# The second group's first tile picks its experts in three steps between its lists

## The chip, the cores and the metric

The kernel runs on one core of one Trainium2 chip. Its metric is the device time of one execution in microseconds (us); less is better. A core has engines with instruction streams of their own: TensorE (PE) for matrix products, VectorE (DVE), ScalarE (ACT), GpSimd (POOL), and SyncE (SP), which here only starts transfers. Sixteen DMA engines move data between the chip's main memory (HBM) and the core's own memory. Here POOL does nothing but start gathered transfers, in which each of 128 partitions fetches a row of its own; SP and ACT start the plain ones.

## The reference, cut to what matters

The reference is one decoder block for 1024 tokens of width 1024. Three token mixers run side by side on a normalised input, are gated and summed, and go through an output projection. A channel mixer follows, in which each token picks 128 experts out of 16384; each expert is one row of `u` and one of `v`:

```python
q = (hf @ w_q).reshape(T, 8, 2, 128)
sc = einsum('thpd,hpkd->thpk', q, subkeys)       # 8 heads x 2 halves x 128 keys
s1, i1 = top_k(sc[:, :, 0], 16)
s2, i2 = top_k(sc[:, :, 1], 16)
cand = (s1[..., :, None] + s2[..., None, :]).reshape(T, 8, 256)
cand_idx = (i1[..., :, None] * 128 + i2[..., None, :]).reshape(T, 8, 256)
top_s, pos = top_k(cand, 16)
idx = take_along_axis(cand_idx, pos, axis=-1)    # 8 x 16 = 128 experts of a token
gate = softmax(top_s)
...
act = gelu(einsum('chkd,cd->chk', u[ic], hc))
out = einsum('chk,chkd->cd', gc * act, v[ic])
```

All of it is float32, and every expert row has 1024 numbers (4096 bytes).

## The kernel before

**Tiles and groups.** The 1024 tokens are eight tiles of 128 (one token per partition), numbered 0 to 7. The dense front (projections, the three mixers, gating, output projection, and the scores of the experts' keys) runs in three groups of 2, 3 and 3 tiles: 0-1, 2-4 and 5-7 (`GROUPS`, line 30; `phase1`, line 1077). "Group 0, 1, 2" below are these. In the code a group is known by its first tile: n0 = 0, 2 or 5.

**Two ways through the experts.** Tiles 4 and 6 (`DENSE`, line 31) take all 16384 experts as a dense product with a matrix of gates; that stage (`dense`, line 1297) comes after the three groups. The other six tiles gather. For each of the 128 chosen experts of a tile, POOL fetches one row of `u` per token (128 rows of 4096 bytes in one instruction, line 1135, called "a row" in the prediction), DVE multiplies it by the token's vector `h` and sums (line 1186), and 34 steps later (`VLAG`) POOL fetches the row of `v`, which PE sums, four at a time, into `poa` and `pob` with weights `wz` (line 1220). `u` has five buffers (`UP`), `v` eight (`VP`), and `h` one (line 1148): the next tile's `h` is loaded over SP when its first row is asked for, once the tile before has no product left.

**The choice.** `select` (line 884) runs at the end of each group. For each of 16 half heads (`hp`) it projects with `w_pq`, forms the scores with the subkeys, copies them to the tile `sc` (or to a `wide` buffer for the second tile of three), and for the group's first tile (for two tiles in the last group) makes the list of the 16 best (`half_list`, `top16`, lines 950 and 875); after every second half head the 112 candidate sums of that head are formed and their 16 best found, with their positions in `pos`. The steps are queued in a small pipe (`Pipe`, line 59), so that the list of `hp` is written two projection steps after its projection. `pick` (line 976) then turns positions into expert numbers: a copy of the indices to float (`f16`), some fifteen small integer and float operations, and one-hot compare, multiply and reduce over eight and over sixteen columns, for each half. `pick` works on a range of heads h0 to h1.

**Stages.** `STAGES` (line 973) cuts the eight heads into three ranges: 0-4, 4-6 and 6-8. In groups 0 and 2 the first tile's ranges are picked inside `select`, as soon as the lists of those heads stand (after hp = 7 and 11); after the first range `begin` (line 906) makes the expert numbers of the first 64 rows and enters the tile in the list `ready` with a limit of 31 rows (`FIRST`, line 47). The last range is picked in `topk` (line 1010), which also makes the gates, turns the indices for the `v` rows and lifts the limit to 128. In group 1 (n0 = 2) `select` only makes the lists of its first tile, tile 2; `topk` picks all eight heads at once, and only at its end tile 2 enters `ready`. The lists of a group's further tiles are made in `topk` as well. `topk` runs as side work, a step now and then, while the next group's front goes on.

**What sets the order.** The loop at lines 1507-1527 weaves three things into one program: steps of the gathered experts (`Experts.step`: a product, a fetch of `v`, sums), steps of the dense front (`fill`), and side work. It keeps two clocks of estimated time, one for PE and one for DMA, and a due time that grows with each expert step, and adds front steps until PE's clock has passed the others. When no expert step is possible it runs a front step, and side work until the next tile is ready. ACT and POOL run in the order in which the program was written; for PE, DVE and SP a scheduler of the framework arranges the instructions by when their inputs are expected.

Of the kernel before, what the change touches and what calls it, by code (L numbers as in the profile page):

```python
# [7 lines left out]
F32 = mybir.dt.float32  # L8
# [11 lines left out]
NT = T // 128  # L20
# [61 lines left out]
def block_kernel(ctx: ExitStack, tc: tile.TileContext, io):  # L82
# [6 lines left out]
    tk = pool("tk", 1)  # L89
# [22 lines left out]
    def bank():  # L112
        return ps.tile([128, 512], F32, name="bank")
# [124 lines left out]
    def load(out, src):  # L238
        count(out)
        nc.sync.dma_start(out, src)  # L240
# [99 lines left out]
    def proj_T(w, h, n):  # L340

        p = bank()
        if type(w) is tuple:
            wh, wl = w
            for k in range(KD):
                hh, hl = (x[:, k % 4, :n] for x in h[1][k // 4])
                mmr(p[:, :n], wh[:, k, :], hh, start=k == 0, stop=False)
                mmr(p[:, :n], wl[:, k, :], hh, start=False, stop=False)
                mmr(p[:, :n], wh[:, k, :], hl, start=False, stop=k == KD - 1)
            return p  # L350
        for piece, o, m in pieces(h[0], n):
            for k in range(KD):
                mm(p[:, o:o + m], w[:, k, :], piece[:, k], start=k == 0, stop=k == KD - 1)
        return p
# [529 lines left out]
    def select(pipe, weights, h2T, n0, G, out):  # L884
        N = G * 128
        sides(9999)
        subk = big.tile([128, 16, 128], F32, name="big")
        load(subk, io["subk"])
        scs = [wide.tile([128, 8 * NMAX], F32, name="wide")[:, :2048].rearrange("p (a b) -> p a b", a=16)
               if G > SUB and i == 1 else sc.tile([128, 16, 128], F32, name="sc") for i in range(G)]  # L890
        lists = [new_lists()]
        last = n0 + G == NT
        if last or n0 == 0:
            early[:] = [tk.tile([128, 8, 2, 16], F32, name="f16")]
        if last:

            a, b = (gm.tile([128, 2, 2, 128], F32, name="ab") for _ in range(2))
            half = lambda t: t.rearrange("p h (a b) -> p (h a) b", b=16)
            early.append(half(b[:, 1]).rearrange("p (h z) b -> p h z b", z=2))
            a, c, b = a[:, 0], a[:, 1], b[:, 0]  # L900
            lists.append((half(a).rearrange("p (h z) b -> p h z b", z=2),
                          half(b).rearrange("p (h z) b -> p h z b", z=2).bitcast(U32),
                          half(c)[:, 0:8], half(c)[:, 8:16].bitcast(U32)))
        entry = {}

        def begin(room, sel, m):
            idx = room[:, 896:896 + m]
            nc.vector.scalar_tensor_tensor(idx, sel[:, 0, :m], 128.0, sel[:, 1, :m], op0=OP.mult, op1=OP.add)
            iI = keep.tile([128, 128], I32, name="iI", bufs=3)
            nc.vector.tensor_copy(iI[:, :m], idx)  # L910
            entry.update(n=n0, iI=iI, have=m, limit=FIRST)
            out.append(entry)

        for hp in range(16):
            p = proj_T(weights("w_pq", hp), h2T, N)
            q = tmp.tile([128, EW], F32, name="e")
            actf(q[:, :N], p[:, :N], AF.Copy)

            def part(hp=hp, q=q):
                z = bank()  # L920
                for i in range(G):
                    mm(z[:, i * 128:(i + 1) * 128], q[:, i * 128:(i + 1) * 128], subk[:, hp, :],
                       start=True, stop=True)
                for i in range(G):
                    actf(scs[i][:, hp, :], z[:, i * 128:(i + 1) * 128], AF.Copy)

            def first(hp=hp):
                for l, x in zip(lists, scs):
                    half_list(hp, x, *l)
                for f, l, x in zip(early, lists, scs):  # L930
                    for h0, h1, at in STAGES[:-1]:
                        if (last or n0 == 0) and hp == 2 * h1 - 1:
                            room = x.rearrange("p a b -> p (a b)")
                            sel = None
                            for sel in pick(room, l, f, h0, h1, at):
                                pass
                            if h0 == 0 and l is lists[0]:
                                begin(room, sel, 16 * h1)
            pipe.tick()
            pipe.push(part, first)  # L940
            next(stores[n0], None)
            yield
        pipe.flush()
        side.append(topk(n0, G, scs, out, lists, entry))

    def new_lists():
        return (tk.tile([128, 8, 2, 16], F32, name="s16", bufs=2), tk.tile([128, 8, 2, 16], U32, name="i16"),
                tk.tile([128, 8, 16], F32, name="ts"), tk.tile([128, 8, 16], U32, name="pos"))
# [23 lines left out]
    early = []  # L972
# [37 lines left out]
    def topk(n0, G, scs, out, lists, entry):  # L1010
        for i in range(G):
            if i >= len(lists):
                l = new_lists()
                for hp in range(16):
                    half_list(hp, scs[i], *l, tied=n0 + G == NT)
                    yield
                    if hp % 2:
                        yield
            else:
                l = lists[i]  # L1020
            s16, i16, ts, pos = l
            room = scs[i].rearrange("p a b -> p (a b)")
            flat = lambda t: t.rearrange("p h a -> p (h a)")
            if i >= len(lists) or 0 < n0 < NT - G:
                f16 = tk.tile([128, 8, 2, 16], F32, name="f16")
                sel = yield from pick(room, l, f16, 0, 8, (1792, 1664, 0, 0, 512, 1536))
            else:
                sel = yield from pick(room, l, early[i], *STAGES[-1])
            idx = room[:, 1024:1152]
            nc.vector.scalar_tensor_tensor(idx, sel[:, 0, :], 128.0, sel[:, 1, :], op0=OP.mult, op1=OP.add)  # L1030
            ge = s16.rearrange("p h a b -> p (h a b)")[:, 0:128].rearrange("p (a b) -> p a b", a=8)
            nc.vector.tensor_sub(ge, ts, ts[:, :, 0:1].to_broadcast([128, 8, 16]))
            actf(ge, ge, AF.Exp)
            sm = room[:, 1152:1160]
            nc.vector.tensor_reduce(sm, ge, AX, OP.add)
            nc.vector.reciprocal(sm, sm)
            shared = sm[:, :, None].to_broadcast([128, 8, 16])
            if n0 + i in DENSE:
                nc.vector.tensor_mul(ge, ge, shared)
            else:  # L1040
                begun = i == 0 and bool(entry)
                t = entry if begun else dict(n=n0 + i, iI=keep.tile([128, 128], I32, name="iI", bufs=3), have=0)
                nc.vector.tensor_copy(t["iI"][:, t["have"]:], idx[:, t["have"]:])
                gk = keep.tile([128, 128], F32, name="gk", bufs=3)
                nc.vector.tensor_mul(gk.rearrange("p (a b) -> p a b", a=8), ge, shared)
            for _ in range(LAG):
                yield
            pt = pg.tile([128, 512], F32, name="pt") if behind[0] else bank()
            if n0 + i in DENSE:
                flip(pt[:, 0:128], sel[:, 0, :])  # L1050
                flip(pt[:, 128:256], sel[:, 1, :])
                flip(pt[:, 256:384], flat(ge))
                sl = gm.tile([128, 3, 128], F32, name="sl", bufs=1)
                actf(sl, pt[:, :384].rearrange("p (a b) -> p a b", a=3), AF.Copy)
                chosen.append(sl)
                stored.append(n0 + i)
                yield
                continue

            for i4 in range(4):  # L1060
                turn(pt[:, i4 * 32:i4 * 32 + 32], idx[:, 32 * i4:32 * i4 + 32])
            iT = keep.tile([128, 4, QB, 4], I32, name="iT", bufs=3)
            nc.vector.tensor_copy(iT.rearrange("p c j i -> p i c j"),
                                  pt[:, :128].rearrange("p (i c j) -> p i c j", i=4, c=4))
            t.update(gk=gk, iT=iT, limit=128)
            if not begun:
                out.append(t)
            yield
# [388 lines left out]
    def sides(n):  # L1457
        while n and side and not wait[0]:
            if next(side[0], 0) == 0:
                side.pop(0)  # L1460
            n -= 1
# [122 lines left out]
```

## Time and profile before

| what | value |
|---|---|
| median of 3 runs | 3554.88 us (3551.26 to 3556.88) |
| the profiled execution | 3549.93 us |
| its span | 3548.2 us |
| instructions in the span | 56579 |
| mean granted clock of TensorE | 0.942 |
| read from HBM / written | 1140.61 MB / 37.75 MB |
| mean DMA rate over the span | 332 GB/s |

The profile is of one execution. Its page gives the busy time of each engine (PE for matrix products, PEld for their weight loads), the DMA queues, and the chain of work that ended last, followed back from the end. Finer views are used beside it: a timeline of one engine's instructions (start, duration, engine, line, operation, output and inputs, and in brackets the idle time before it and what ended that), groups of equal instructions (count, busy time, mean duration in ns), and stretches of the span with each engine's busy time. Names of tiles lose their numbers there: `i` is `i16`, `s` is `s16`, `f` is `f16`. Each matrix product of float32 appears as more than one record.

### The profile page before, as it was taken

What the parts mean: (1) busy time and instruction counts of PE and PEld (TensorE: products, weight loads), DVE (VectorE), ACT (ScalarE), POOL (GpSimd) and SP (SyncE); (2) the same over time, 40 slices, a digit from 0 to 9 for tenths busy, and PEclk for the clock granted to TensorE, in tenths of its full rate; (3) what the DMA queues carried; (4) which work ended last, traced back from release to release, by engine and by line L of the source; (5) the groups of instructions that cost most, each with busy time, mean ns of one, the idle gap of its engine ahead of it and who ended that gap; (6) DMA issues with size and microseconds to landing.
All of it is one profiled execution on the core that took longest, in us unless ns stands there. A gap on an engine that the chain in (4) does not pass through costs nothing.

```text
span 3548.2 us, 56579 instructions
## 1 busy us (share of the span) xinstructions
PE 3134.6 (88%) x21218; PEld 2270.9 (64%) x21218; DVE 2304.0 (65%) x5883; ACT 1015.4 (29%) x2075; POOL 1745.9 (49%) x1543
## 2 busy tenths in 40 slices
PE   7999968899899899899998999886768888898998
PEld 5889835566455476566664555565547777787876
DVE  6544587565544457888666665578759766667673
ACT  4543213332200111344222111112223333333332
POOL 0000045564567654667665665444754645354653
PEclk9999989999999999999999999988989999999999
DMA  4435677898899998899998999988998999999997
GB/s 169 122 104 178 220 280 279 308 401 319 298 372 400 409 392 320 308 330 344 400 334 309 376 397 385 403 299 311 400 382 334 372 407 388 377 386 409 406 404 293
DMA packets 344611, 1182.13 MB, mean 333 GB/s; under 512 B 38481, under 2 KB 81489, under 8 KB 324881
## 3 DMA queue, kind: packets, MB, share of 16 engines
q0 software_dynamic: 221184, 805.40, 59.9%
q1 hardware_dynamic: 100848, 336.37, 25.5%
q10 hardware_dynamic: 22304, 36.74, 2.8%
q8 instruction: 167, 2.74, 0.3%
q14 instruction: 108, 0.88, 0.1%
HBM read 1140.61 MB, written 37.75 MB: 332 GB/s over the span
## 4 chain that ended last, share of the span: by engine, by line
PE 51%; DMA 15%; DVE 12%; issue 12%; POOL 6%; ACT 2%; another core or an unknown queue 1%; ACTq 0%; SPq 0%; POOLq 0%; DVEq 0%
PE bank L120 33%; PE bank L1241 10%; DMA u<-in_u,iI 8%; DMA v<-in_v,iT 4%; PE poa L1220 4%; DVE u L1186 4%; POOL v L1135 3%; PE pob L1220 3%; POOL u L1135 3%; PE bank L124 1%; DMA ur<-in_uT 1%; ACT e L131 1%; DVE sc L880 0%; DVE ab L1271 0%
## 5 line engine op out<-in xcount | busy, mean ns | idle before, releaser
L1135 POOL DMA_INDIRECT u<-in_u,iI x768 | 876.8, 1142 | 961.3 <-DVE pos L879 437.6
L1186 DVE SCALAR_TENSOR_TENSOR u<-u,h 128x1024 f32<-128x1024 f32 x768 | 932.5, 1220 | 514.2 <-DMA u<-in_u,iI 428.9
L1135 POOL DMA_INDIRECT v<-in_v,iT x768 | 868.3, 1131 | 805.7 <-PE pob L1220 319.1
L120 PE MATMUL bank<-wide,w 128*128 128x384 f32 x1536 | 520.9, 492 | 3.1 <-DVE wide L816 3.0
L120 PEld LDWEIGHTS bank<-wide,w 128*128 128x128 f32 x1536 | 290.5, 192 | 208.8 <-issue 21.0
L1241 PE MATMUL bank<-hh,pu 128*128 128x256 f32 x1200 | 234.6, 295 | 37.6 <-ACT w L131 28.5
L1220 PE MATMUL poa<-v,wz 128*32 128x256 f32 x3072 | 220.0, 410 | 45.2 <-DMA v<-in_v,iT 24.9
L1241 PE MATMUL bank<-pv,wh 128*128 128x512 f32 x712 | 232.4, 407 | 23.0 <-DVE pv L1336 12.0
L131 ACT ACTIVATE e<-bank 128x512 f32<-128x512 f32 (+2 forms) x208 | 110.1, 529 | 486.0 <-PE bank L120 345.8
L120 PE MATMUL bank<-w,wide 128*128 128x128 f32 (+1 forms) x1056 | 221.6, 367 | 25.6 <-DVE wide L336 23.4
L120 PE MATMUL bank<-big,w 128*128 128x256 f32 (+1 forms) x1280 | 237.7, 343 | 2.5 <-issue 2.5
L1220 PE MATMUL pob<-v,wz 128*32 128x256 f32 x3072 | 205.7, 399 | 36.8 <-DVE u L1186 17.1
L1241 PEld LDWEIGHTS bank<-hh,pu 128*128 128x128 f32 x1200 | 201.6, 202 | 52.2 <-ACT w L131 31.1
L120 PEld LDWEIGHTS bank<-big,w 128*128 128x128 f32 x1280 | 207.9, 194 | 30.7 <-issue 9.8
L120 PEld LDWEIGHTS bank<-w,wide 128*128 128x128 f32 x1056 | 143.7, 193 | 99.9 <-issue 66.7
L1220 PEld LDWEIGHTS poa<-v,wz 128*32 128x32 f32 x3072 | 97.3, 116 | 140.2 <-issue 47.0
L1220 PEld LDWEIGHTS pob<-v,wz 128*32 128x32 f32 x3072 | 96.4, 113 | 125.8 <-issue 47.3
L1241 PE MATMUL bank<-hl,pu 128*128 128x256 f32 x600 | 175.7, 293 | 0.0
L1241 PEld LDWEIGHTS bank<-pv,wh 128*128 128x128 f32 x712 | 131.5, 193 | 59.9 <-DVE pv L1336 14.3
L131 ACT ACTIVATE w<-bank 128x256 f32<-128x256 f32 x128 | 48.7, 381 | 385.1 <-PE bank L1241 244.1
L120 PE MATMUL bank<-oT,w 128*128 128x384 f32 (+1 forms) x480 | 153.6, 459 | 2.5 <-DMA w<-in_w_o 2.5
L1241 PE MATMUL bank<-u 128*128 128x256 f32 (+1 forms) x464 | 146.6, 316 | 9.6 <-ACT u L131 9.6
(306 smaller groups left out, 5565.3 us busy)
## 6 DMA issues: line engine op xcount, KB each, us to landing
ur<-in_uT SPq DMA_DIRECT2D x64, 1024.0 KB
vr<-in_vd SPq DMA_DIRECT2D x64, 1024.0 KB
w<-in_w_in SPq DMA_DIRECT2D x90, 512.0 KB
w<-in_w_gate SPq DMA_DIRECT2D x72, 512.0 KB
w<-in_w_pq SPq DMA_DIRECT2D x48, 512.0 KB
g<-gd SPq DMA_DIRECT2D x16, 1024.0 KB
w<-in_w_o SPq DMA_DIRECT2D x48, 256.0 KB
w<-in_w_out SPq DMA_DIRECT2D x24, 512.0 KB
```

The costliest lines, as they stand in the source:

```text
L120: nc.tensor.matmul(out, lhsT, rhs, **kw)
L124: nc.tensor.transpose(out, in_, ident)
L131: nc.scalar.activation(out, in_, f, **kw)
L1135: nc.gpsimd.indirect_dma_start(out=t, out_offset=None, in_=io[kind], in_offset=bass.IndirectOffsetOnAxis(ap=ap, axis=0))
L1186: nc.vector.scalar_tensor_tensor(u, u, 1.0, t["h"], op0=OP.mult, op1=OP.mult, accum_out=t["parts"][:, k:k + 1])
L1220: nc.tensor.matmul(o[32 * k:32 * k + 32], t["wz", c][:, x, :], vs[y][:, 256 * k:256 * k + 256], start=b == 0 and x == SUMS - 1 and c % 2 == 0,
L1241: nc.tensor.matmul(out, lhsT, rhs, **kw)
```

## The change

Three conditions fall. Every group now has the buffer `f16` in `early` and picks its first tile's heads 0-4 and 4-6 inside `select`, with `begin` behind the first of them; `topk` picks the last two heads of every first tile and uses the pick of all eight heads at once only for tiles whose lists it makes itself. For groups 0 and 2 nothing is different: there the old conditions were true already. What is left is group 1: tile 2 gets its choice in three steps, and enters `ready` with a limit of 31 rows after the first.

```diff
         lists = [new_lists()]
         last = n0 + G == NT
-        if last or n0 == 0:
-            early[:] = [tk.tile([128, 8, 2, 16], F32, name="f16")]
+        early[:] = [tk.tile([128, 8, 2, 16], F32, name="f16")]
         if last:
...
                 for f, l, x in zip(early, lists, scs):
                     for h0, h1, at in STAGES[:-1]:
-                        if (last or n0 == 0) and hp == 2 * h1 - 1:
+                        if hp == 2 * h1 - 1:
...
             s16, i16, ts, pos = l
             room = scs[i].rearrange("p a b -> p (a b)")
             flat = lambda t: t.rearrange("p h a -> p (h a)")
-            if i >= len(lists) or 0 < n0 < NT - G:
+            if i >= len(lists):
                 f16 = tk.tile([128, 8, 2, 16], F32, name="f16")
                 sel = yield from pick(room, l, f16, 0, 8, (1792, 1664, 0, 0, 512, 1536))
             else:
                 sel = yield from pick(room, l, early[i], *STAGES[-1])
```

## The prediction

> **What bounds the kernel now.** The page comes first. TensorE is busy for 88% of the span and is half of the chain that ended last; the rest of the chain is mostly the fetches of expert rows and what handles them.
>
> ```profile
> PE 3134.6 (88%) x21218; PEld 2270.9 (64%) x21218; DVE 2304.0 (65%) x5883; ACT 1015.4 (29%) x2075; POOL 1745.9 (49%) x1543
> q0 software_dynamic: 221184, 805.40, 59.9%
> PE 51%; DMA 15%; DVE 12%; issue 12%; POOL 6%; ACT 2%; another core or an unknown queue 1%; ACTq 0%; SPq 0%; POOLq 0%; DVEq 0%
> ```
>
> The software queue moves 805.40 MB in 1536 fetches, so one gathered row set (one instruction on POOL, "a row" below) is 0.524 MB. Averages don't decide this change; the place does. So the second view is POOL's timeline at the border between tile 1 and tile 2.
>
> ```profile
> 1338.06 0.94 POOL L1135 DMA_INDIRECT u<-in_u,iI  x1 [0.30 <-issue]
> 1339.30 1.83 POOL L1135 DMA_INDIRECT v<-in_v,iT  x1 [0.30 <-issue]
> ...
> 1426.08 0.94 POOL L1135 DMA_INDIRECT v<-in_v,iT  x1 [0.30 <-issue]
> 1427.33 0.94 POOL L1135 DMA_INDIRECT u<-in_u,iI  x1 [0.31 <-issue]
> ...
> 1504.94 0.94 POOL L1135 DMA_INDIRECT v<-in_v,iT  x1 [0.31 <-issue]
> ```
>
> Tile 1's last u row leaves at 1338.06 and tile 2's first at 1427.33. Between them POOL fetches v rows only; from 1427.33 to 1504.94 it fetches u rows only. POOL never runs dry: at 1427 u follows v after the usual 0.31 us. The 89.3 us hole in u is no hole in the fetching, which is the caution in all that follows. The third view is the busy time by stretches cut at those times (columns: length, busy time of PE, weight loads, DVE, ACT, POOL with instruction counts, granted clock, DMA share, GB/s).
>
> ```profile
> 1250.00:1338.00 88.00, 81.98 (x607) 67.51 (x606) 48.12 (x170) 12.85 (x43) 42.18 (x42) 0.94 1.01 391
> 1338.00:1427.00 89.00, 82.06 (x568) 51.84 (x568) 68.90 (x332) 12.92 (x36) 43.70 (x40) 0.96 0.88 316
> 1427.00:1505.00 78.00, 66.91 (x390) 45.28 (x388) 66.86 (x149) 31.54 (x56) 47.77 (x41) 0.96 0.85 300
> 1505.00:1600.00 95.00, 89.01 (x560) 60.35 (x564) 84.33 (x258) 46.07 (x77) 64.88 (x55) 0.95 0.92 332
> ```
>
> POOL's count is the number of rows: 42, 40, 41 and 55. PE idles for 6.0, 6.9, 11.1 and 6.0 us. In the two middle stretches the DMA engines have room (shares 0.88 and 0.85 against 1.01 before), yet PE is still 92% and 86% busy. So PE is the nearer wall, and what PE idles there above its habit is what can be had on the spot.
>
> **The change part by part.** *What starts earlier.* Of tile 2's lists, the eighth (head 3, second half) and its candidates end on DVE at 1327.2; today the choice waits for the sixteenth and runs from 1380.40 to 1404.1.
>
> ```profile
> 1326.95 0.27 DVE L882 FIND_INDEX8 pos<-ts,sc 128x8 uint32<-128x112 f32 x1
> ...
> 1380.40 0.29 DVE L982 CAST f<-i 128x256 f32<-128x256 uint32 x1
> ...
> 1403.88 0.24 DVE L1043 CAST iI<-sc 128x128 int32<-128x128 f32 x1
> ```
>
> In group 0, which already works by steps, the first step took from 422.62 to 435.21 between other lists, 12.6 us.
>
> ```profile
> 422.62 0.22 DVE L982 CAST f<-i 128x128 f32<-128x128 uint32 x1
> ...
> 435.02 0.19 DVE L910 CAST iI<-sc 128x64 int32<-128x64 f32 x1
> ```
>
> So tile 2's first indices stand at about 1327.2 + 12.6 = 1339.8, just as tile 1's u ends. The step runs two projection steps after its list was begun, so tile 2 is in the ready list before tile 1 is used up, and u and v go on in turns across the border. Thirty-one u rows at half of 42 rows in 88 us last 130 us, to about 1470; the other half of the choice, late today at 1404, is there by then, and if it isn't the loop forces it (lines 1520-1526).
>
> *What moves.* No row is added. PE's price of a row is read in the select loop (columns: start, us, what):
>
> ```profile
> 1283.07 5.69 PE L120 MATMUL bank<-big,w 128*128 128x256 f32 x32
> 1288.60 0.83 PE L120 MATMUL bank<-big,e 128*128 128x128 f32 x6
> 1289.27 5.40 PE L120 MATMUL bank<-big,w 128*128 128x256 f32 x32
> 1294.51 0.83 PE L120 MATMUL bank<-big,e 128*128 128x128 f32 x6
> 1295.28 1.93 PE L1220 MATMUL poa<-v,wz 128*32 128x256 f32 x32
> ...
> 1357.72 1.93 PE L1220 MATMUL pob<-v,wz 128*32 128x256 f32 x32
> 1359.59 5.50 PE L120 MATMUL bank<-big,w 128*128 128x256 f32 x32
> ```
>
> Four v rows cost PE 1.93 us, a u row nothing: 0.24 us a row on average. With u and v in turns four sums stand behind two projection steps; in the v-only time behind each one. So after the change PE is through the last seven steps about 7 us sooner, and owes those sums in the u-only time, where it idles most. Its sum of work is the same. *On the spot* the gain is idle time: at the neighbours' 7% (6.0 of 88) the stretches would idle 6.2 and 5.5 us instead of 6.9 and 11.1, that is 6.3 us less. The ends are 0 and 6.3 us; I take **4**, nearer the upper, since the u-only time packs 41 row products into 78 us of a DVE that is 86% busy, and the change halves them there.
>
> *The lead.* With both streams the first stretch carries 42/88 = 0.477 rows per us and the last 55/95 = 0.579; the middle ones 0.449 and 0.526. Raised to their neighbours they carry 2.5 + 4.1 = 7 rows more, so expert work stands 7 rows ahead from there on. The ends: 0 rows, or, if the DMA engines fill to 391 GB/s, (75 x 89 + 91 x 78) us x GB/s = 13.8 MB = 26 rows. What a row is worth when it falls away at the end is read there:
>
> ```profile
> 3434.00:3512.00 78.00, 72.65 (x550) 52.52 (x547) 37.19 (x57) 21.94 (x35) 40.07 (x39) 0.98 1.00 390
> 3512.00:3548.00 36.00, 27.32 (x158) 19.92 (x156) 12.44 (x17) 8.18 (x12) 1.22 (x2) 0.93 0.44 168
> ```
>
> At 390 GB/s a row takes 1.34 us, if DMA is the wall; 0.24 us, if PE is. Seven rows are 1.7 to 9.4 us. PE is 93% busy there, so I take **4**, in the lower half.
>
> *What is added on DVE.* One step of eight heads handles 512 and 1024 elements in its one-hot operations; three steps handle 256 and 512, then twice 128 and 256 (the smallest forms take the shortest time of the row).
>
> ```profile
> L1002 DVE TENSOR_TENSOR sc<-sc,iota x40: 270/548/1219, 426.8 to 2749.4; 128x256 f32<-128x256 f32 x12, 128x512 f32<-128x512 f32 x12, 128x128 f32<-128x128 f32 x8, 128x1024 f32<-128x1024 f32 x8
> L1002 DVE TENSOR_TENSOR sc<-sc,iota 128x512 f32<-128x512 f32 x12 | 8.2, 681 | 0.0
> L1002 DVE TENSOR_TENSOR sc<-sc,iota 128x256 f32<-128x256 f32 x12 | 4.9, 412 | 0.0
> L986 DVE TENSOR_SCALAR sc<-pos x10: 175/186/361, 424.5 to 2734.3; 128x32 f32<-128x32 uint32 x4, 128x128 f32<-128x128 uint32 x4, 128x64 f32<-128x64 uint32 x2
> ```
>
> Each step has six operations of either size (compare, multiply and reduce, twice; all three take alike). Before: 6 x (0.68 + 1.21) = 11.3 us. After: 6 x (0.41 + 0.68) + 2 x 6 x (0.27 + 0.41) = 14.7. The sixteen small operations run three times instead of once, 32 more at 0.18 = 5.8, and two more make the first indices. DVE gets about 9.6 us more, 3% of what it does in these 350 us. Its cover is DVE's idle time, 40 us in the first stretch and 20 in the second; without cover it would cost up to 9.6. The shorter third step also takes some 7 us out of today's burst at 1380-1404, in which PE once waits for the choice:
>
> ```profile
> 1388.65 1.93 PE L1220 MATMUL poa<-v,wz 128*32 128x256 f32 x32 [1.86 <-DVE sc L1004]
> ```
>
> I take **+1**.
>
> *The wait that is added.* The tile h has one buffer: tile 2's can only load when tile 1's last product is done. Today that hides in the 89 us. At the two borders that run through, DVE waited for it:
>
> ```profile
> 1832.35 1.23 DVE L1186 SCALAR_TENSOR_TENSOR u<-u,h 128x1024 f32<-128x1024 f32 x1 [4.50 <-DMA h<-h2s]
> 2884.07 1.23 DVE L1186 SCALAR_TENSOR_TENSOR u<-u,h 128x1024 f32<-128x1024 f32 x1 [4.96 <-DMA h<-h2s]
> ```
>
> Around these waits PE was busy as follows (the columns of the stretches above):
>
> ```profile
> 1820.00:1840.00 20.00, 19.96 (x138) 12.54 (x138) 14.05 (x25) 4.75 (x11) 10.46 (x11) 1.00 1.00 389
> 2860.00:2880.00 20.00, 15.19 (x104) 12.85 (x104) 13.73 (x21) 8.51 (x15) 7.00 (x6) 0.83 1.03 405
> ```
>
> Behind it on DVE stand the next lists; on POOL a u row finds its five buffers full and holds the v rows behind it, for which PE's sums wait; on SP the h load holds the weight loads behind it, which are two steps ahead. PE lost nothing at 1832 and at most 4.8 us around 2870. I take **+1**, near the first, which is in the same phase.
>
> *The sum:* -4 - 4 + 1 + 1 = **-6 us**. On the profiled execution (3549.9 us, of which 3548.2 are its span) that is 3543.9; the median of the three runs shown is 4.95 us above that execution, so the forecast is 3554.9 - 6 = **3549 us**. The runs shown lie between 3551.3 and 3556.9; 0.2%, or 7.1 us, is about what a measurement can tell from no change.
>
> **The rivals.**
>
> *More comes of it.* The DMA room is filled further: 26 rows at 0.24 to 1.34 us are 6 to 35 us; with the whole spot gain of 6 and the two costs of 2 that is 10 to 39 us less, 3516 to 3545, say **3532**. For it speak the shares of 0.88 and 0.85; against it PE, 92% busy in the first of these stretches, and DVE.
>
> *PE is the wall everywhere.* The sums only change places, and u rows brought into the select loop just share the queues: 0 us, **3555** (3551 to 3558). For it speaks that in 1250-1338, with both streams at DMA share 1.01, PE idles 7% as it does in the v-only time. The Trainium skill says so as a rule (DMA: Bandwidth & Descriptors, "Issuing engines are not separate DMA queues"): transfers started by any engine run on the same 16 DMA engines and interleave, so the early u rows take their time from v rows and weights. By that rule alone the sum is 0; the trace agrees where the share is 1.01, not where it is 0.88.
>
> *Slower: DVE overflows.* The stretch 1338-1427 has 68.9 us of DVE work in 89. Four products u x h run there now, the first and last of them below. The change brings some 17 more (half of 42, less these), at 1.22 + 0.08 us, and up to 9.6 us of choice.
>
> ```profile
> 1339.11 1.22 DVE L1186 SCALAR_TENSOR_TENSOR u<-u,h 128x1024 f32<-128x1024 f32 x1
> 1340.25 0.08 DVE L1186 DVE_READ_ACCUMULATOR u<-u,h 128x1 f32 x1
> ...
> 1346.78 1.21 DVE L1186 SCALAR_TENSOR_TENSOR u<-u,h 128x1024 f32<-128x1024 f32 x1
> ```
>
> ```profile
> L1186 DVE SCALAR_TENSOR_TENSOR u<-u,h 128x1024 f32<-128x1024 f32 x768 | 932.5, 1220 | 514.2 <-DMA u<-in_u,iI 428.9 <-issue 72.4 <-DMA h<-h2s 9.5
> ```
>
> That is 68.9 + 22.1 + 9.6 = 100.6, 12 us too much. It decides from 89 us on, if the lists of tile 3 can't slip: late products keep u buffers, POOL holds the v rows behind them, PE's sums wait. Price: up to 12 us and 4.8 for h, less the lead of 4: up to +13, 3562 to 3568, say **3566**. Against it: the lists of tile 3, which fill the end of that stretch, are needed late and can slip into the next, which loses as many products as this one gains.
>
> *It doesn't do what it says.* If the scheduler of DVE places the first step late, the first u row still comes after 1400: 3555 to 3558.
>
> **How the numbers follow.** Forecast (3543 to 3552) 0.42; more comes of it 0.18; PE is the wall 0.17; slower 0.18; not as said 0.05. Faster by over 0.2% (under 3547.8): the whole of the second and half of the first (0.21), 0.39. Slower (over 3562): 0.18. Within: 0.43. The range leaves out the far half of the gain case and the far part of the slower one: 3530 to 3566.
>
> **What would show it.** Right: tile 2's first u row at about 1340 to 1350 and its first v row hardly earlier than 1505; DMA share over 0.92 in both stretches; a wait of about 5 us for h near 1350; PE idle under 7 us in 1427-1505; the last v row some 10 us before 3512. Wrong: PE waits for v or DVE near 1350 to 1400 (slower); row counts there unchanged (no lead); an end that keeps its length although the rows end earlier (the lead is worth nothing).

## The result, and the profile after

The changed kernel took 3583.5 us against 3551.2 us of the kernel before (medians of six runs each): a ratio of 1.0091, with a 95% interval from 1.0072 to 1.0111, so about 32 us slower. The forecast was 3549 us with a range from 3530 to 3566. Kernels of one series of runs share a chip. The kernel before took about 3552 or 3580 us in some series and 3456 us in two others, so ratios here are always to the kernel before of the same series. By the chip numbers on record the two series near 3456 us ran on chips 7 and 15, called "the faster chips" below; the others ran on chips 6, 10 and 13, "the slower chips" (chip 10 twice, at 3584 and at 3552 us). The comparison that gave the result has no number; by its time it belongs to the slower ones.

The page of the changed kernel, its busy line and the chain that ended last:

```profile
PE 3158.7 (88%) x21218; PEld 2286.7 (64%) x21218; DVE 2306.2 (64%) x5941; ACT 1015.7 (28%) x2075; POOL 1739.1 (49%) x1543
PE 46%; DMA 16%; issue 14%; DVE 12%; POOL 7%; another core or an unknown queue 2%; ACT 2%; ACTq 0%; POOLq 0%; SPq 0%; DVEq 0%
```

The number of matmuls is the same, and TensorE is busy 24 us longer with them (between two traces of one kernel it differs by 16 us too). "issue" has 14% of the chain instead of 12%, but that is no trait of the change: a second trace of the kernel before has 14% as well. DVE's busy time rises by 2.2 us. The choice itself costs more than that: the operations of `pick` for tile 2 last 15.5 us together in the kernel before and 24.7 us in the changed one, 9.2 us more, as the prediction had it. POOL's timeline (start, us, what, idle before):

```profile
1338.91 1.14 POOL L1134 DMA_INDIRECT u<-in_u,iI  x1 [1.72 <-DVE u L1185]
...
1343.51 1.85 POOL L1134 DMA_INDIRECT u<-in_u,iI  x1 [2.22 <-DVE ts L876]
...
1494.37 1.80 POOL L1134 DMA_INDIRECT v<-in_v,iT  x1 [0.41 <-PE pob L1219]
...
3515.09 0.94 POOL L1134 DMA_INDIRECT v<-in_v,iT  x1 [0.30 <-PE bank L1240]
```

The change does what it says. Tile 1's last u row leaves at 1338.9, and tile 2's first at 1343.5 instead of 1427.3. Its first v row leaves at 1494.4 instead of 1504.9, and the hole in u is gone. The wait for h is there too, in DVE's waits between 1338 and 1427:

```profile
DVE u L1185 <- DMA h<-h2s: 4.4, 1, 4.4
```

The stretches of the prediction, with the same cuts, after the change:

```profile
1338.00:1427.00 89.00, 81.27 (x455) 50.91 (x454) 81.30 (x336) 14.61 (x39) 52.87 (x47) 0.96 0.94 359
1427.00:1505.00 78.00, 67.02 (x433) 43.06 (x432) 59.96 (x191) 27.83 (x48) 44.54 (x39) 0.87 0.81 289
1505.00:1600.00 95.00, 79.22 (x518) 53.02 (x516) 78.95 (x304) 33.53 (x58) 55.00 (x49) 0.91 0.86 304
```

In the first, 47 rows go instead of 40, at a DMA share of 0.94. But the next two carry 39 and 49 rows where they carried 41 and 55; the granted clock falls to 0.87 and 0.91, and the DMA share to 0.81 and 0.86. Equal times are unfair here, since the two kernels stand at different work. So the second view cuts at equal progress: where the 6000th, 6250th, 7000th and 9000th and the last matmul of the front start (all matmul records but those of the sums of v rows, counted from 0). The kernel before, then the changed one:

```profile
1354.74:1447.45 92.71, 81.71 (x571) 45.79 (x569) 71.33 (x329) 12.77 (x32) 45.92 (x42) 0.93 0.86 312
1447.45:1624.02 176.57, 163.55 (x975) 112.89 (x976) 159.32 (x453) 82.62 (x141) 118.70 (x101) 0.97 0.90 321
1624.02:2039.71 415.69, 383.28 (x2930) 244.40 (x2929) 272.80 (x589) 122.56 (x286) 261.25 (x233) 0.97 0.95 355
2039.71:3543.31 1503.60, 1301.89 (x9019) 1011.38 (x9017) 1019.62 (x2427) 426.10 (x829) 792.37 (x684) 0.93 0.96 374
```

```profile
1353.95:1436.87 82.92, 72.06 (x411) 41.42 (x410) 76.17 (x330) 13.56 (x34) 48.54 (x45) 0.95 0.95 371
1436.87:1650.01 213.14, 186.56 (x1200) 123.15 (x1200) 172.28 (x527) 82.88 (x140) 122.66 (x109) 0.91 0.83 290
1650.01:2087.68 437.67, 391.37 (x2929) 251.32 (x2928) 260.83 (x571) 121.88 (x285) 253.62 (x234) 0.93 0.91 341
2087.68:3573.48 1485.80, 1297.38 (x8955) 1009.52 (x8953) 1011.08 (x2408) 426.22 (x829) 782.95 (x671) 0.93 0.96 373
```

The select loop is 9.8 us shorter. It has 160 matmuls fewer, five groups of sums at 1.93 us: 9.7 us, all of them put off. So nothing is gained there. The stick-breaking stage of group 2, which comes next (6250 to 7000), is 36.6 us longer. Seven groups of sums more (225 matmuls) explain 13.6 of that; 23 us are new. Up to the 9000th matmul another 22.0 us are lost with an equal number of matmuls. The rest of the program is 17.8 us shorter, with the expert rows ahead by two groups of four sums. Together -9.8 + 36.6 + 22.0 - 17.8 = +31 us. The question is where the 23 and the 22 us come from.

### The profile page after: what moved, and what is told of

Its sections match the earlier page's. It is cut to its first block, busy times and chain, and to the rows that moved or that the text cites. A ratio compares the mean times of both kernels' runs of the same rounds, so it can differ in the third digit from the quotient of the medians.

```text
span 3578.3 us, 56641 instructions
## 1 busy us (share of the span) xinstructions
PE 3158.7 (88%) x21218; PEld 2286.7 (64%) x21218; DVE 2306.2 (64%) x5941; ACT 1015.7 (28%) x2075; POOL 1739.1 (49%) x1543
## 4 chain that ended last, share of the span: by engine, by line
PE 46%; DMA 16%; issue 14%; DVE 12%; POOL 7%; another core or an unknown queue 2%; ACT 2%; ACTq 0%; POOLq 0%; SPq 0%; DVEq 0%
PE bank L120 30%; PE bank L1240 9%; DMA u<-in_u,iI 8%; DMA v<-in_v,iT 5%; POOL v L1134 4%; DVE u L1185 4%; PE poa L1219 3%; POOL u L1134 3%; PE pob L1219 3%; PE bank L124 1%; ACT e L131 1%; DMA g<-gd 1%; DVE sc L880 0%; DVE pu L1335 0%
## 5 line engine op out<-in xcount | busy, mean ns | idle before, releaser
L1134 POOL DMA_INDIRECT v<-in_v,iT x768 | 859.6, 1119 | 777.8 <-PE poa L1219 303.9
L1219 PE MATMUL poa<-v,wz 128*32 128x256 f32 x3072 | 212.2, 400 | 31.3 <-DVE wz L1209 17.6
```

The lines of the kernel that those rows point to most:

```text
L1134: nc.gpsimd.indirect_dma_start(out=t, out_offset=None, in_=io[kind], in_offset=bass.IndirectOffsetOnAxis(ap=ap, axis=0))
L1219: nc.tensor.matmul(o[32 * k:32 * k + 32], t["wz", c][:, x, :], vs[y][:, 256 * k:256 * k + 256], start=b == 0 and x == SUMS - 1 and c % 2 == 0,
```

## The experiments

Three theories stood at first: "crowding" (late sums and early rows stand between the short chains of group 2's front), "DVE" (the work of the three steps), "order" (any shift of the written program costs as much).

**First and third series: parts of the change.** The three steps alone (the tile joins the ready list in `topk`, as before):

```diff
-                            if h0 == 0 and l is lists[0]:
+                            if h0 == 0 and l is lists[0] and (last or n0 == 0):
                                 begin(room, sel, 16 * h1)
```

> The second group's first tile gets its choice in three steps, but joins the ready list only when the last step is done, as in the kernel before. Theory 'crowding' (the loss of 32 us comes from the rows and sums that the early start moves into the front of the third group): about the kernel before, 3545 to 3560. Theory 'DVE' (the extra and differently placed DVE work of the three steps costs the time): 3570 to 3590. Theory 'order' (any shift of the written order moves the time by as much, with no one place): no fixed number, anything from 3530 to 3590, with the difference to the kernel before spread over the whole span.

> Three steps of the choice, tile joins only when all are done. On the first series' chip 1.0023 [1.0005, 1.0041]. Crowding: 0.999 to 1.004 here too, and well under the changed kernel. DVE: as the changed kernel, 1.006 to 1.011.

Joining three projection steps later:

```diff
-            out.append(entry)
+            if last or n0 == 0:
+                out.append(entry)
...
+                if 0 < n0 < NT - G and hp == 13:
+                    out.append(entry)
```

> As the changed kernel, but the tile joins the ready list three projection steps later (after the lists of head 6), about 40 us later, so that roughly half of the u rows that the change moves still move. Crowding: about half of the loss, 3560 to 3572. DVE: the whole loss, 3577 to 3590. Order: no fixed number.

> Tile joins three projection steps later. On the first series' chip 1.0012 [0.9991, 1.0034]. Crowding: between the kernel before and the changed one, 1.002 to 1.006. DVE: 1.006 to 1.011.

A pause of the expert work, once, where group 2 begins:

```diff
             due = max(due + least, pe - least)
+            if group[0] == 2 and not held[0]:
+                held[0] = True
+                due += 24000.0
```

> As the changed kernel, but where the third group begins the expert work is held once for 24 us of the planner's time (about 7 u and 7 v rows), so that the lead is given up there and the rows after it stand against the third group about as in the kernel before. Crowding, in the form 'the lead packs too much beside the front of the third group': 3555 to 3568. If the loss is made by the sums that are owed at the border, whatever the lead: 3575 to 3590, and the end of the span longer by the rows given back. DVE: 3583 or more.

> The changed kernel with the expert work held for 24 us of planner's time where the third group begins. On the first series' chip 1.0029 [1.0014, 1.0045]. Lead packs too much beside the front: 1.001 to 1.005, under the changed kernel. Sums owed at the border, whatever the lead: 1.006 to 1.011.

A control on the kernel before, and the two kernels themselves again:

```diff
-LEAST = 1500.0
+LEAST = 1550.0
```

> Control: the kernel before with the planner's least spacing of expert steps 1550 instead of 1500 per stream, a change of 3% that has nothing to do with the choice. Crowding or DVE: within 10 us of the kernel before, 3541 to 3561, since the spacing decides only where the front has little work. Order: 15 us or more off it on either side, with the difference wandering along the span.

> The changed kernel once more, this time on one chip with the three kernels of the first series (chips differ: 3457 us for the kernel before in the first series, 3551 and 3584 us elsewhere). Loss belongs to the program on any chip: ratio 1.006 to 1.011. Loss belongs to slow chips only, and this is a fast one (kernel before near 3457): 0.998 to 1.004.

Ratios to the kernel before of the same series, with intervals:

```
                 chip 7 (3457)             chip 13 (3581)
changed kernel   not run                   1.0105 [1.0085, 1.0125]
three steps      1.0023 [1.0005, 1.0041]   1.0034 [1.0016, 1.0052]
join later       1.0012 [0.9991, 1.0034]   1.0039 [1.0013, 1.0065]
pause            1.0029 [1.0014, 1.0045]   1.0050 [1.0021, 1.0078]
LEAST 1550       0.9998 [0.9983, 1.0014]   not run
```

So "DVE" falls as the cause of the whole: the steps alone cost a third of it on the slower chip. Some two thirds come only when the tile joins at once, and joining 40 us later or a pause takes most of them away; that is what crowding expected. The control moved nothing, but it ran on chip 7 alone, so "order" isn't ruled out on the slower chips.

**Second series: short sums.** The sums multiply 64 of 256 columns, in both kernels.

```diff
-                    nc.tensor.matmul(o[32 * k:32 * k + 32], t["wz", c][:, x, :], vs[y][:, 256 * k:256 * k + 256],
+                    nc.tensor.matmul(o[32 * k:32 * k + 32, :64], t["wz", c][:, x, :], vs[y][:, 256 * k:256 * k + 64],
```

> The sums of v rows multiply only 64 of each 256 columns, in the kernel before (three quarters of the columns of v are left out of the output; every fetch, product and wait stays). 192 groups of four sums shrink from 1.93 us to about 0.6 us: up to 250 us of TensorE work less. It is the base of short_after.

> The same short sums (three quarters of the columns of v left out) in the changed kernel. Crowding (the sums owed at the border stand between the short chains of the third group's front): the loss shrinks with the sums to a third or less, ratio to short_before 0.996 to 1.003. Order or DVE: the loss stays, ratio 1.006 to 1.011.

> The changed kernel again, with nothing else changed, beside the other kernels of this series on one chip. The kernel before took 3457 us in the first series against 3551 us in the comparison that gave the result, so the chip, or its state, differs by 2.7%. If the loss belongs to the program: 0.7 to 1.1% over the kernel before, as it was. If it belongs to the chip of the first comparison (slower transfers there, or a lower granted clock): within 0.4%.

> The kernel before again, for a trace on this chip: ratio 1.000 within 0.2%. If the chip is the faster one, what is shorter than in the first trace (granted clock, DMA durations) says what a slower chip lacks.

The kernel before again: 0.9982 [0.9963, 1.0000]; the changed one: 1.0079 [1.0052, 1.0106]. With short sums the kernel before came to 3556.0 us, 0.9923 [0.9892, 0.9954], the changed one to 3533.9 us, 0.9864 [0.9832, 0.9896]: its loss of 26 us had turned into a gain of 22. To each other that is 0.994, a gain beyond the 0.996 to 1.003 that crowding had been given. The direction agreed with crowding, but the traces don't put the gain where crowding has it: from the 6000th to the 9000th matmul the two short kernels take 738.7 and 737.3 us, and the gain lies behind them.

**Fourth series: only the border.** Short sums for rows 200 to 299 alone; the wait for h taken away; the three steps done together in `topk`.

```diff
+                m = 64 if 200 <= self.sums < 300 else 256
                 for k in range(4):
-                    nc.tensor.matmul(o[32 * k:32 * k + 32], t["wz", c][:, x, :], vs[y][:, 256 * k:256 * k + 256],
+                    nc.tensor.matmul(o[32 * k:32 * k + 32, :m], t["wz", c][:, x, :], vs[y][:, 256 * k:256 * k + m],
```

> In the kernel before, the sums of rows 200 to 299 only (25 groups of four) multiply 64 of 256 columns; the other columns of v are left out there. TensorE has 25 x 1.3 = 33 us less to do around the border. Base of near_after; by all theories 5 to 30 us under the kernel before.

> The same short sums (rows 200 to 299, three quarters of the columns left out there) in the changed kernel. Crowding at the border (late sums beside the short chains): the loss mostly goes, ratio to near_before 0.997 to 1.004. Loss spread over the span, or made by the DVE work: ratio to near_before 1.007 to 1.011.

```diff
-                    h = gw.tile([128, D], F32, name="h", bufs=1)
-                    nc.sync.dma_start(h, h2s[n])
+                    if n != 2:
+                        self.h = gw.tile([128, D], F32, name="h", bufs=1)
+                        nc.sync.dma_start(self.h, h2s[n])
+                    h = self.h
```

> The changed kernel, in which tile 2 keeps the h of tile 1 (its own h is not loaded and so is left out of its products), so that the first product of tile 2 waits for no h at the border. If the wait for h has a part in the loss: ratio to the kernel before 1.002 to 1.006. If not: 1.008 to 1.011, as the changed kernel.

> The changed kernel, tile 2 keeping tile 1's h (its own is not loaded and left out of its products). On a slower chip (kernel before over 3540 us): if the wait for h makes the loss beyond the three steps, 1.002 to 1.005; if not, 1.007 to 1.011. On the faster chip again: 1.002 to 1.005, which leaves it open.

```diff
+                if n0 and i < 1:
+                    for s in STAGES[:-1]:
+                        for _ in pick(room, l, f16, *s):
+                            pass
+                    sel = yield from pick(room, l, f16, *STAGES[-1])
```

> The kernel before, with the second group's first tile choosing in the same three steps, but one behind the other where the single choice stood. If the added DVE work costs by itself: 1.002 to 1.004, as the three steps between the lists did (1.0023 and 1.0034). If it is the place between the lists: 0.999 to 1.001.

> The changed kernel once more. On a slower chip (kernel before over 3540 us): 1.007 to 1.011 as before. On the faster one (kernel before near 3456): if the loss from joining early belongs to the order of work itself, 1.007 to 1.011 too; if it comes from what the slower chips add to it, 1.002 to 1.005, like the kernel without the h wait (1.0037) and the three steps alone (1.0023 and 1.0030).

This series fell on a faster chip (number 15, 3455 us): near_before 0.9983 [0.9968, 0.9998], near_after 1.0001 [0.9984, 1.0019], by the medians 1.0025 to each other. As the changed kernel itself never ran there, that decides nothing between crowding and the rest. steps_together 1.0030 [1.0013, 1.0046]: the steps cost about the same in one place as between the lists, so their place isn't the matter. h_kept 1.0037 [1.0021, 1.0054] there, and in a later series on a slower chip (3552 us) 1.0140 [1.0107, 1.0173]. So the wait for h doesn't make the loss: without it the kernel lost at least as much there as the changed kernel did in its four comparisons (0.75% to 1.05%). The changed kernel came to 1.0075 [1.0045, 1.0104] in a fourth comparison, on a slower chip again.

**What the same program shows on the two chips.** h_kept is the changed kernel but for one load, and has a trace from either chip. ACT's timeline at the same instructions in group 2's stick-breaking, on the faster chip and on the slower one:

```profile
1490.68 0.58 ACT L131 ACTIVATE e<-bank 128x512 f32<-128x512 f32 x1
1494.29 0.60 ACT L131 ACTIVATE e<-bank 128x512 f32<-128x512 f32 x1 [3.03 <-PE bank L120]
```

```profile
1550.00 0.58 ACT L131 ACTIVATE e<-bank 128x512 f32<-128x512 f32 x1
1558.39 0.60 ACT L131 ACTIVATE e<-bank 128x512 f32<-128x512 f32 x1 [7.81 <-remote]
```

On the faster chip ACT waits 3.03 us for PE; on the slower one 7.81, and the view names no releaser ("remote" is its word for another core or an unknown queue, and there is no other core here). The changed kernel itself stops at this instruction for as long in its traces on the slower chips, here the first and the second:

```profile
1558.20 0.60 ACT L131 ACTIVATE e<-bank 128x512 f32<-128x512 f32 x1 [7.83 <-remote]
```

```profile
1560.23 0.60 ACT L131 ACTIVATE e<-bank 128x512 f32<-128x512 f32 x1 [7.91 <-remote]
```

PE's timeline around it, h_kept on the faster chip and then the changed kernel:

```profile
1491.68 1.94 PE L1221 MATMUL poa<-v,wz 128*32 128x256 f32 x32
1493.54 0.65 PE L120 MATMUL bank<-e,oT 128*64 128x128 f32 x6
...
1496.39 1.05 PE L120 MATMUL bank<-qpad,big 128*128 128x128 f32 x8
1497.37 0.44 PE L120 MATMUL bank<-e,oT 128*64 128x128 f32 x4
```

```profile
1550.79 1.93 PE L1219 MATMUL poa<-v,wz 128*32 128x256 f32 x32
1552.65 0.65 PE L120 MATMUL bank<-e,oT 128*64 128x128 f32 x6
...
1555.49 1.05 PE L120 MATMUL bank<-qpad,big 128*128 128x128 f32 x8
1560.65 0.44 PE L120 MATMUL bank<-e,oT 128*64 128x128 f32 x4 [4.11 <-ACT e L131]
```

From the sums to the qpad products PE takes 4.71 and 4.70 us: the two run alike to a hundredth. ACT starts 2.61 us after the sums on one chip and 7.41 us after them on the other, 4.8 us later on the same input, and PE then stands for 4.1 us. It is no late row, no product of DVE and no sum: what PE waits for is ACT, and ACT waits for PE's signal. The trace also keeps the events of the semaphores, the counters by which one engine tells another that an instruction is done. For seven instructions of PE that give a signal, one behind the other, here is the end, the signal (both in us, paired in order) and how long it came behind the end in the changed kernel's first trace, and last the same delay in h_kept on the faster chip:

```
                    end      signal   behind   behind, h_kept
poa<-v,wz           1551.86  1552.25   0.39    0.04
poa<-v,wz           1552.29  1553.75   1.46    0.05
poa<-v,wz           1552.72  1556.66   3.94    0.04
bank<-e,oT          1553.30  1558.11   4.81    0.01
bank<-S,none        1555.22  1558.21   2.98    0.01
bank<-sp,none       1555.66  1558.25   2.59    0.01
bank<-qpad,big      1556.55  1558.34   1.80    0.01
```

ACT starts 0.08 us after the fourth signal, on the faster chip 0.08 us after the same one. The last four signals come within 0.23 us, though their matmuls ended over a stretch of 3.2 us. So it is the signals that are held back, and not the matmuls (the ends of matmuls in a trace are modelled, so how long each was held is rough). The view says "remote" because no instruction of PE that gives a signal had ended shortly before.

Waits without a known releaser can be counted. In the waits of DVE and ACT, the idle time that ended in "issue" or "remote" between the 6000th and the 9000th matmul of the front (columns "stops", in us), beside the length of the two stretches and, last, of the rest of the program:

```
slower chips          6000-7000     7000-9000     9000 to the end
                      us   stops    us   stops    us
kernel before         269   15      416   50      1504
kernel before, again  280   28      427   82      1513
changed, 1st trace    296   61      438  118      1486
changed, again        297   43      446   97      1497
changed, third        297   46      440  151      1493
changed, fourth       297   58      444  115      1490
h_kept_2              301   70      437  110      1500
steps_only_2          294   48      440  117      1506
join_later_2          283   36      443  109      1503
pause_2               279   38      446  126      1502
faster chips
least_before          265    0      399    5      1485
steps_only            273    0      400   11      1495
steps_together        265    0      405   10      1482
join_later            256    0      402    0      1488
pause                 266    0      403    4      1485
h_kept                268    0      394    4      1486
```

(The idle time before a stop's end holds some ordinary waiting too, 3 us of the 7.8 above, so the columns show how much stands there, not a price.) The label also takes in waits whose signal the record lacks: the traces of the slower chips hold only 3350 to 3460 signals of DVE for some 4200 to 4270 instructions that give one, those of the faster chips nearly all. A narrower count doesn't depend on that. It takes only the waits of ACT and DVE, labelled "remote", that ended with a signal of PE on record, more than 1.5 us after the last instruction of PE that gives one had ended. Between 6000 and 9000 they hold 31 and 51 us in the two traces of the kernel before, 90 to 122 us in the four of the changed one, 110 us in h_kept_2, and none in any trace of the faster chips.

On the slower chips the first stretch is longer where more stops stand: 269 us at 15, 294 to 301 us at 43 to 70. In the second that holds only between the two kernels (416 and 427 us against 438 to 446); in the changed kernel's traces 151 us of stops stand at 440 us and 97 at 446. The two short kernels don't fit at all: in the second stretch they have 168 and 80 us of stops at 435 and 440 us. The row steps_only_2 is of that kernel's slowest run, 20 us over its median. On the faster chips there are next to no stops, and the loss of 49 us between 6000 and 9000 (-9.8 + 36.6 + 22.0) isn't there. LEAST 1550 (chip 7), which stands for the kernel before, and h_kept (chip 15), for the changed one, at equal progress:

```profile
1303.90:1388.85 84.95, 78.04 (x571) 44.30 (x569) 67.64 (x321) 12.90 (x32) 40.61 (x40) 0.94 0.90 333
1388.85:1568.47 179.62, 164.70 (x985) 113.81 (x976) 162.75 (x462) 82.58 (x141) 126.26 (x103) 0.95 0.90 323
1568.47:1967.89 399.42, 375.52 (x2931) 242.14 (x2930) 274.47 (x593) 122.61 (x286) 255.60 (x231) 0.97 0.97 371
```

```profile
1310.77:1388.31 77.54, 67.21 (x412) 40.30 (x413) 71.48 (x312) 14.24 (x37) 50.30 (x43) 0.96 0.96 363
1388.31:1579.13 190.82, 177.28 (x1222) 117.44 (x1208) 175.74 (x551) 82.34 (x138) 135.02 (x112) 0.96 0.93 336
1579.13:1973.50 394.37, 371.75 (x2930) 240.59 (x2929) 260.77 (x571) 121.62 (x285) 253.07 (x234) 0.99 0.99 380
```

-7.4, +11.2 and -5.0 us: -1.2 in all. (The pair with short sums at the border, near_before and near_after, both on chip 15, takes 655.8 and 660.7 us between 6000 and 9000, 4.9 us apart.) The sums that were put off cost 11.2 us there, somewhat less than their own length (237 matmuls, 14.3 us). So crowding alone falls: without the stops, late sums and early rows fit beside the short chains. The same program says it without a stand-in: between 6000 and 9000, h_kept takes 663 us on the faster chip and 738 us on the slower one, 75 us more, where the kernel before stands only 21 and 43 us over LEAST 1550.

## Why the prediction was wrong

The sign was wrong. The step that failed is one that the sum leaves at nothing: "Its sum of work is the same" was taken to mean that sums which are put off cost no time where they go, and that nothing is lost in the stages behind the border. It held for the number of matmuls. In time, those stages lost 23 + 22 = 45 us in the trace of the result, beyond the length of the sums, and the sum has no term for them. On the faster chips the moved sums did fit, as the step has it. A second, smaller step failed on both: the three steps of the choice cost more than the +1 that was put down. Term by term:

- **Spot gain, forecast -4.** The select loop ended 9.8 us sooner, and 9.7 of that were put-off sums. The idle time that was to take in the put-off sums gave nothing: between the 6250th and the 7000th matmul they came with 23 us of new time.
- **Lead, forecast 7 rows and -4.** In rows it came out as forecast: in every trace of the changed kernel eight rows more are summed at the 7000th and at the 9000th matmul. In time the program behind the 9000th is 17.8 us shorter on the slower chips, but not on the faster ones (h_kept 1486 us, LEAST 1550 1485), so how much of the 17.8 us the lead is worth isn't shown. It pays back less than half of what was lost ahead of it. The last v row still leaves at 3515, since the loss ahead of it eats the lead, and 63 us of dense work follow it instead of 36.
- **DVE's added work, forecast +9.6 us of work and +1 of time.** The work was sized rightly (9.2 us), though DVE's busy time as a whole rises by only 2.2 us. The time was not: the three steps alone cost 0.23 to 0.34%, 8 to 12 us, between the lists on either kind of chip and together on a faster one. The cover of idle time that the forecast counted on didn't hold; why isn't settled.
- **Wait for h, forecast 4.5 to 5.0 us on DVE and +1 of time.** It came with 4.4 us, and without it nothing was won. The forecast read one bound, 4.8 us, from the stretch 2860 to 2880, which ends 0.9 us into that wait (2879.1 to 2884.1); within the wait PE was busy throughout.

Of the rivals, "PE is the wall everywhere" saw that the sums only change places, but not the loss. "Slower: DVE overflows" had the sign, but not the place or the mechanism: the stretch in which DVE should have overflowed is the one that became shorter, and the one wait of PE for DVE there is 4.3 us for an operation of the choice at 1392, 2.4 us longer than the 1.86 us that the kernel before shows at that point. Its price of up to 13 us fell short by 19. Of the marks, the first u row, the first v row and the wait for h came as forecast. A DMA share over 0.92 held in one stretch of two, PE idles 11.0 us in 1427-1505 instead of under 7, and the last v row wasn't earlier.

What the runs put in place of the failed step: on the slower chips, ACT and DVE wait at some instructions for signals of PE that come microseconds late. Of the "remote" waits between the 6000th and the 9000th matmul, some 24 in a trace, seven fall on the same instruction in all four traces of the changed kernel and in h_kept_2; others fall in one trace alone. In the kernel before, fewer such waits fall there (31 and 51 us against 90 to 122). In group 2's stick-breaking PE, ACT and DVE work in a chain, as at 1558: a late signal of PE holds ACT, and PE then stands for 4.1 us itself.

Shown is that the 45 us belong to the slower chips, and that the two kernels differ there in how much waiting stands behind late signals. It is no strict rule: pause_2 has 129 us of such waits and loses only 0.5% in all, and the two short kernels, with 178 and 62 us, take 738.7 and 737.3 us. So three things stay open. Why the changed order meets more late signals was not tested, nor why joining later or a pause loses less. What makes the signals late was not tried; since the same traces lack a fifth of DVE's signals, the recording may have a part in it. And the changed kernel itself never ran on a faster chip; h_kept stood for it there.

The page that the prediction started from had one small sign of this: "another core or an unknown queue" held 1% of the chain that ended last, where no other core runs, and no page of the faster chips has that entry. "issue" with its 12% is no sign: on the faster chips, where the 45 us are missing, it holds 13% (LEAST 1550) and 14% (h_kept).

## What to carry to other kernels

Work that is moved has to be priced where it goes, from rows of that place. Compare kernels at equal progress and on more than one chip: an effect of 1% of a reordering may belong to the chip as much as to the order. Where a trace knows no releaser of a wait, look at the times of the signals themselves before calling the wait causeless: the signal can be late, or missing from the record. None of the complete versions tried here beat the kernel before.

## What was not expected of the hardware

The same kernel took 3456 us in some series and 3552 to 3584 us in others. In the kernel before DVE has 104 and 125 us of waits that end in "issue" on the slower chips, and its near twin (LEAST 1550) 0 on the faster one; with a fifth of DVE's signals missing from the slower chips' traces, part of that is the record. The 167 instruction transfers of 16 KB are the same, with like times for each (1.05, 1.03 and 1.04 us on average): so transfers of instructions that take longer are not the reason.

PE's signals differ most. On the slower chips 475 to 636 of PE's 2108 to 2157 signals on record come more than 0.12 us after the last instruction of PE that gives one had ended; on the faster chips 8 to 35 of some 2310 do. The signals of ACT and DVE that are on record are almost all on time on both kinds of chip; what the missing ones did can't be seen.

A pause of PE costs more than its length. PE's timeline of the changed kernel before and after a pause of 4.7 us:

```profile
1461.01 0.60 PE L120 MATMUL bank<-sp,ntri 128*128 128x256 f32 x2
...
1469.63 1.12 PE L120 MATMUL bank<-e,big 128*64 128x256 f32 x4 [4.73 <-ACT e L131]
...
1471.28 1.06 PE L120 MATMUL bank<-sp,ntri 128*128 128x256 f32 x2
```

The same pair of matmuls takes 1.06 us instead of 0.60. The Trainium skill (TensorE: Matmul & The Clock Gate, "Part 1: The HAM clock gate") says that the array falls to half its clock after an idle window of about 3.4 us and gets it back after such a window of work; this trace agrees in kind, its clock record standing at half from 1465.67 to 1475.91 us. That stretch at half clock and one from 1434.95 to 1445.19 are why the granted clock of 1427-1505 fell from 0.96 to 0.87. Over the whole span the clock stands at half for 476 us, against 413 and 450 us in the two traces of the kernel before, which goes with the 24 us that PE is "busy" longer with the same matmuls.
